# A hybrid attention and delta-rule encoder layer: zero fills on VectorE, some stores and loads issued by ScalarE

## The chip, the core and the metric

The kernel runs on one core of a Trainium2 chip. The metric is the device time of one execution in microseconds (us); less is better. A core has five engines with a queue of instructions each, and each takes its own in order: TensorE (PE, with its weight loads as PEld), VectorE (DVE), ScalarE (ACT), GpSimd (POOL) and SyncE (SP). They wait for each other by semaphores. Transfers (DMA) are issued by an engine and run beside it; SP does nothing else than issue them.

## The reference

One trunk layer on x of 1 x 1024 x 1024 in float32:

```
h   = x + W_out( concat[ windowed attention , gated DeltaNet both ways ] )( RMSNorm(x) )
h   = h + W2 relu(W1 RMSNorm(h))^2
out = RMSNorm_final(h)
```

The attention has 8 query heads and 2 key heads of 64, a window of 128 around each token, and a relative bias from a small table. The DeltaNet has 4 heads of 128, chunks of 64 tokens, and two directions. For each chunk and head it needs the inverse of a unit triangular matrix of 64 x 64 (`t_mat`, below), and then runs a recurrence over the chunks:

```
a_mat = where(strict, beta * kk * decay, 0)
t_mat = triangular_solve(eye + a_mat, eye)
v_new = u - w @ state ;  o = q @ state + qk @ v_new ;  state = state * exp(gl) + k^T @ v_new
```

## The kernel before

The sequence of 1024 tokens is worked on in chunks of 128 (eight, NT) or halves of 512 (HALF). Large gemms (`mm3`, L124 to L126) split each float32 operand into a high part, which is the value rounded to a shorter mantissa, and the low rest, and add three products; `split` (L119 on ACT, L120 on POOL) makes the parts.

The work is written as Python generators (projections, inversion, attention, scan, output, feed-forward) which are woven together. At build a planner then lays every instruction out in one order on each engine, by its own estimate of the times. So an edit of a line, which changes what that line costs in the plan, can move other instructions on every engine, also far behind it. Buffers come from rings: `pg` (128 x 1024), `pt` (128 x 512), `wr`, `wh`, `wl`, `sc`, and the PSUM banks `psA` and `psB`. A number behind such a name is the buffer's place in the program.

What stands around the change:

- `proj_attn` ends with the queries: for each key head kv, two pieces i of the heads and two halves, a gemm into psA, L494 (DVE, scale), L495 (ACT, high part qh), L496 (POOL, low part), and then four stores of 128 KB each into `qad` in HBM (L500): two of the high part, two of the low. There are 32 stores. `query(n, kv)` (L594) reads a chunk of the queries of one key head back, issued by POOL; `attention` uses it in L544 and L545 on PE, followed by the softmax (L546, L553 to L563) and its transposes (L573, L575, L585). Its bias tiles come by L529 from `biasd`.
- The triangular matrices are inverted in blocks. The innermost, 32 x 32, is an elimination on DVE (L675 and L677, then L686 and L687). `invert(tt, steps)` joins the blocks to 64 x 64, for each of four steps i and both directions d. A step loads two tiles of `atd` (L707, 512 KB each), clears two tiles of `tt` (L710), copies the diagonal blocks in (L714, ACT) and then goes back and forth between PE and a copy: L720 (PE), L723 (ACT), L730 and L734 (PE), L739 and L746 (DVE), L744 (ACT), L753 (PE), L755 (ACT), L761 (PE), L764 (DVE).
- `scan` (from L780; its first matmul is L797) begins when the first tiles are inverted.
- Later, `out_gdn(c)` norms the DeltaNet's output of chunk c: squares on ACT (L900), five small operations (L902 to L906, the last on POOL), L907 (DVE, writes a `wr`), L910 (four transposes on PE), L911 (DVE). `out_gemm` multiplies the result by W_out (L124 to L126, added to h by L876). Beside it `tokens_second` makes the second half of the normed tokens: L209 (transposes on PE), L214 and L966 (ACT), L215 and L970 (DVE), L949 (ACT) and L950 (DVE or POOL).

Of the kernel before, what the change touches and what calls it, by code (L numbers as in the profile page):

```python
# [21 lines left out]
HALF = 512  # L22
# [55 lines left out]
class Block:  # L78
# [383 lines left out]
    def proj_attn(self):  # L462


        nc = self.nc
        w = self.io["w_in"][0]
        raws = self.load_w(self.w_cols(w, C_AK, 256))
        lo, up = slice(0, 64), slice(64, 128)
        self.kh, self.kl = [self.pg(dt=F32R) for _ in range(2)], [self.pg(dt=F32R) for _ in range(2)]
        for v, o in enumerate((up, lo)):  # L470
            nc.vector.tensor_copy(out=self.kl[v][o, :], in_=self.zero[o, :].to_broadcast([64, SEQ]))
        self.va = self.pg((P, NT, P))
        for i, half, ps in self.pair(raws):
            tok = slice(half * HALF, (half + 1) * HALF)
            t = self.pt()
            nc.vector.tensor_copy(out=t, in_=ps)
            if i == 0:
                swap = self.pt()
                nc.sync.dma_start(out=swap[up, :], in_=t[lo, :])
                nc.sync.dma_start(out=swap[lo, :], in_=t[up, :])  # L480
                for v, (r, o) in enumerate(((lo, up), (up, lo))):
                    nc.scalar.copy(out=self.kh[v][r, tok], in_=t[r, :])
                    nc.scalar.copy(out=self.kh[v][o, tok], in_=swap[o, :])
                    nc.gpsimd.tensor_tensor(out=self.kl[v][r, tok], in0=t[r, :], in1=self.kh[v][r, tok].bitcast(F32),
                                            op=ALU.subtract)
            else:
                pv = self.transposed(t, 0)
                nc.vector.tensor_copy(out=self.va[:, 4 * half:4 * half + 4, :], in_=pv)
            yield 5.2
        for kv in range(2):  # L490
            raws = self.load_w(self.w_cols(w, C_AQ + 256 * kv, 256))
            for i, half, ps in self.pair(raws):
                q, qh = self.pt(), self.pt(dt=F32R)
                nc.vector.tensor_scalar(out=q, in0=ps, scalar1=0.125, scalar2=None, op0=ALU.mult)  # L494
                nc.scalar.copy(out=qh, in_=q)  # L495
                nc.gpsimd.tensor_tensor(out=q, in0=q, in1=qh.bitcast(F32), op=ALU.subtract)  # L496
                for part, t in enumerate((qh.bitcast(F32), q)):
                    o = 64 * (kv ^ part)
                    for g in range(2):
                        nc.sync.dma_start(out=self.qad[kv, 2 * i + g, o:o + 64, half * HALF:(half + 1) * HALF],  # L500
                                          in_=t[64 * g:64 * g + 64, :])
                if i == 1 and half == 0:
                    self.qs.append(self.query(0, kv))
                yield 5.2
# [186 lines left out]
    def invert(self, tt, steps):  # L691


        nc = self.nc
        blk = lambda q: slice(32 * q, 32 * q + 32)
        ct, ctt = self.ct, self.ctt
        pairs = (((0, 1), (2, 3)), ((1, 0), (3, 2)))
        sub = ((0, 1), (3, 2))
        lo, hi = slice(0, 64), slice(64, 128)
        ends = ((lo, hi), (hi, lo))  # L700
        flat = lambda a: a.rearrange("p c h x -> p (c h) x")
        for i in steps:
            ns = slice(8 * i, 8 * i + 8)
            at = []
            for d in range(2):
                a = self.pg((P, 2, GH, P))
                nc.sync.dma_start(out=a, in_=self.atd[2 * i:2 * i + 2, :, d].rearrange("c p h x -> p c h x"))  # L707
                at.append(flat(a))
                tt[d][i] = self.pg((P, 2, GH, P)) if d or i < 2 else (self.wl if i % 2 else self.wh)((P, 2, GH, P), F32)
                nc.gpsimd.memset(tt[d][i].rearrange("p c h x -> p (c h x)"), 0.0)  # L710
            t = [flat(tt[d][i]) for d in range(2)]
            for d in range(2):
                for q in range(4):
                    nc.scalar.copy(out=t[d][blk(q), :, blk(q)], in_=ctt[d][blk(q), :, ns].rearrange("p x n -> p n x"))  # L714
            px = self.ps("psB", (P, 8, 32))
            for n in range(8):
                for j in range(2):
                    for d in range(2):
                        s, e = pairs[d][j]
                        nc.tensor.matmul(px[blk(e), n, :], at[d][blk(s), n, blk(e)], ct[d][blk(s), :, 8 * i + n],  # L720
                                         start=True, stop=True)
            x32 = self.pt((P, 8, 32))
            nc.scalar.copy(out=x32, in_=px)  # L723
            yield 1.4
            pyt, py = self.ps("psB", (P, 8, 32)), self.ps("psB", (P, 8, 32))
            for n in range(8):
                for j in range(2):
                    for d in range(2):
                        s, e = pairs[d][j]
                        nc.tensor.matmul(pyt[blk(s), n, :], x32[blk(e), n, :], ctt[d][blk(e), :, 8 * i + n],  # L730
                                         start=True, stop=True)
                for d in range(2):
                    e = sub[d][1]
                    nc.tensor.matmul(py[blk(e), n, :], ctt[d][blk(e), :, 8 * i + n], x32[blk(e), n, :],  # L734
                                     start=True, stop=True)
            t64 = self.pt((P, 8, 64))
            for d in range(2):
                for s, e in pairs[d]:
                    nc.vector.tensor_scalar(out=t[d][blk(s), :, blk(e)], in0=pyt[blk(s)], scalar1=-1.0, scalar2=None,  # L739
                                            op0=ALU.mult)  # L740
                a, b = sub[d]
                for q in (a, b):
                    c = slice(32 * (q % 2), 32 * (q % 2) + 32)
                    nc.scalar.copy(out=t64[blk(q), :, c], in_=ct[d][blk(q), :, ns].rearrange("p x n -> p n x"))  # L744
                nc.gpsimd.memset(t64[blk(a), :, 32 * (b % 2):32 * (b % 2) + 32], 0.0)
                nc.vector.tensor_scalar(out=t64[blk(b), :, 32 * (a % 2):32 * (a % 2) + 32], in0=py[blk(b)], scalar1=-1.0,  # L746
                                        scalar2=None, op0=ALU.mult)
            yield 2.4
            px = self.ps("psB", (P, 8, 64))
            for n in range(8):  # L750
                for d in range(2):
                    s, e = ends[d]
                    nc.tensor.matmul(px[e, n, :], at[d][s, n, e], t64[s, n, :], start=True, stop=True)  # L753
            xs = self.pt((P, 8, 64))
            nc.scalar.copy(out=xs, in_=px)  # L755
            yield 1.8
            py = self.ps("psB", (P, 8, 64))
            for n in range(8):
                for d in range(2):
                    s, e = ends[d]  # L760
                    nc.tensor.matmul(py[s, n, :], xs[e, n, :], t[d][e, n, e], start=True, stop=True)  # L761
            for d in range(2):
                s, e = ends[d]
                nc.vector.tensor_scalar(out=t[d][s, :, e], in0=py[s], scalar1=-1.0, scalar2=None, op0=ALU.mult)  # L764
            yield 1.8
# [612 lines left out]
```

## Time and profile before

| what | value |
|---|---|
| median of 3 runs | 1255.21 us (1253.97 to 1259.02) |
| the profiled execution | 1255.02 us |
| its span, first to last instruction | 1253.3 us |
| mean granted TensorE clock | 0.983 |
| busy: PE, PEld, DVE, ACT, POOL | 1191.6, 967.2, 854.9, 621.4, 580.3 us |
| DMA | 187.62 MB, 150 GB/s over the span |
| L710, eight memsets on POOL | 954 to 1088 ns each, from 263.0 to 346.5 us |
| L500, 32 stores issued by SP | 572 ns each in the median, from 298.8 to 342.0 us |
| L707, eight loads issued by SP | 438 ns each in the median, from 257.5 to 343.4 us |

Times in the views are microseconds from the start of the span; "idle before" or a pair in square brackets is how long an engine had stood before an instruction, and what ended that. `x4` is a count of instructions. A name as `pg<-atd` is what is written and what it is read from. A transfer has two times: that which its issue takes on the issuing engine, and that from the issue to its landing.

### The profile page before, as it was taken

What the parts mean: (1) busy time and instruction counts of PE and PEld (TensorE: products, weight loads), DVE (VectorE), ACT (ScalarE), POOL (GpSimd) and SP (SyncE); (2) the same over time, 40 slices, a digit from 0 to 9 for tenths busy, and PEclk for the clock granted to TensorE, in tenths of its full rate; (3) what the DMA queues carried; (4) which work ended last, traced back from release to release, by engine and by line L of the source; (5) the groups of instructions that cost most, each with busy time, mean ns of one, the idle gap of its engine ahead of it and who ended that gap; (6) DMA issues with size and microseconds to landing.
All of it is one profiled execution on the core that took longest, in us unless ns stands there. A gap on an engine that the chain in (4) does not pass through costs nothing.

```text
span 1253.3 us, 18527 instructions
## 1 busy us (share of the span) xinstructions
PE 1191.6 (95%) x6482; PEld 967.2 (77%) x6482; DVE 854.9 (68%) x1528; ACT 621.4 (50%) x1347; POOL 580.3 (46%) x488
## 2 busy tenths in 40 slices
PE   7999999899789989998999999999999999999997
PEld 5778777677568868877788888888777888888885
DVE  5667667982389986676655454544668797886976
ACT  6455688335485752125464554545545434444343
POOL 5354211362432433144573534535445665655595
PEclk9999999899889999998999999999999999999999
DMA  7134344441956678122234344443678624434323
GB/s 239 52 121 133 101 171 140 139 126 40 223 168 158 190 216 296 60 84 85 84 131 159 132 151 143 154 159 134 223 280 280 223 85 167 151 121 148 95 90 135
DMA packets 121630, 187.62 MB, mean 150 GB/s; under 512 B 11043, under 2 KB 64416, under 8 KB 121537
## 3 DMA queue, kind: packets, MB, share of 16 engines
q1 hardware_dynamic: 96708, 152.58, 37.9%
q10 hardware_dynamic: 16381, 29.67, 6.3%
q0 software_dynamic: 8448, 4.20, 1.9%
q8 instruction: 51, 0.84, 0.3%
q14 instruction: 42, 0.34, 0.1%
HBM read 122.39 MB, written 63.49 MB: 148 GB/s over the span
## 4 chain that ended last, share of the span: by engine, by line
PE 49%; DVE 6%; DMA 3%; issue 2%; POOL 1%; ACT 1%; ACTq 0%; POOLq 0%; DVEq 0%; SPq 0%
PE psA L124 8%; PE psA L125 8%; PE psA L126 8%; PE psB L126 7%; PE psB L125 7%; PE psB L124 7%; DMA pg<-sd 3%; PE psB L797 2%; DVE pg L1154 1%; DVE pt L1163 1%; DVE wr L1166 1%; PE psB L209 1%; DVE pg L1199 1%; DMA sd<-pt 0%; DVE wr L1161 0%
## 5 line engine op out<-in xcount | busy, mean ns | idle before, releaser
L124 PE MATMUL psA<-pg,wh 128*128 128x512 f32 x416 | 167.6, 404 | 2.1 <-ACT pt L458 2.1
L126 PE MATMUL psA<-pg,wl 128*128 128x512 f32 x416 | 166.9, 401 | 0.0
L125 PE MATMUL psA<-pg,wh 128*128 128x512 f32 x416 | 166.5, 400 | 0.0
L120 POOL TENSOR_TENSOR wl<-wr,wh 128x512 fp32r<-128x512 f32 x44 | 70.2, 1618 | 154.0 <-ACT wh L119 153.9
L1154 DVE TENSOR_TENSOR pg<-pg 128x512 fp32r<-128x512 f32 x112 | 122.7, 1127 | 18.8 <-ACT pg L1153 18.6
L120 POOL TENSOR_TENSOR wh<-wr,wh 128x512 fp32r<-128x512 f32 x32 | 47.9, 1518 | 131.5 <-ACT wh L119 131.5
L1071 ACT ACTIVATE pt<-pt 128x512 f32<-128x512 f32 x64 | 40.4, 632 | 122.7 <-DVE pt L1061 122.7
L125 PE MATMUL psA<-pg,pg 128*128 128x512 f32 x256 | 99.7, 391 | 0.5 <-POOL pg L120 0.5
L124 PE MATMUL psA<-pg,pg 128*128 128x512 f32 x256 | 99.0, 391 | 1.0 <-DVE pg L1199 1.0
L126 PE MATMUL psA<-pg,pg 128*128 128x512 f32 x256 | 99.7, 389 | 0.0
L120 POOL TENSOR_TENSOR pg<-wr,pg 128x512 fp32r<-128x512 f32 x48 | 73.4, 1560 | 51.0 <-ACT pg L119 51.0
L124 PEld LDWEIGHTS psA<-pg,wh 128*128 128x128 f32 x416 | 79.2, 190 | 21.3 <-ACT pt L458 2.4
L125 PEld LDWEIGHTS psA<-pg,wh 128*128 128x128 f32 x416 | 79.3, 191 | 19.7 <-issue 0.9
L126 PEld LDWEIGHTS psA<-pg,wl 128*128 128x128 f32 x416 | 79.1, 190 | 18.6
L1153 ACT CAST pg<-pg 128x512 fp32r<-128x512 f32 x112 | 67.2, 620 | 41.3 <-DMA pg<-sd 31.0
L126 PE MATMUL psB<-pg,pg 128*128 128x512 f32 x192 | 75.0, 390 | 1.3 <-DVE pg L1154 1.3
L125 PE MATMUL psB<-pg,pg 128*128 128x512 f32 x192 | 75.0, 391 | 0.8 <-POOL pg L120 0.7
L124 PE MATMUL psB<-pg,pg 128*128 128x512 f32 x192 | 74.7, 390 | 0.4 <-ACT pg L1153 0.4
L119 ACT CAST wh<-wr 128x512 fp32r<-128x512 f32 x76 | 43.6, 623 | 45.5 <-PE psA L125 24.8
L1061 DVE TENSOR_TENSOR pt<-psB,pt 128x512 f32<-128x512 f32 x39 | 26.9, 689 | 55.1 <-PE psB L126 30.1
L1061 DVE TENSOR_TENSOR pt<-psA,pt 128x512 f32<-128x512 f32 x39 | 26.8, 689 | 55.0 <-PE psA L126 39.5
L124 PEld LDWEIGHTS psA<-pg,pg 128*128 128x128 f32 x256 | 48.0, 188 | 12.6 <-DVE pg L1199 2.3
(385 smaller groups left out, 3307.7 us busy)
## 6 DMA issues: line engine op xcount, KB each, us to landing
sd<-pt ACTq DMA_DIRECT2D x112, 256.0 KB, 2.2
pg<-sd SPq DMA_DIRECT2D x112, 256.0 KB, 2.9
wr<-in_w_ffn_in SPq DMA_DIRECT2D x32, 512.0 KB, 3.8
wr<-in_w_in SPq DMA_DIRECT2D x22, 512.0 KB, 4.8
pg<-in_x SPq DMA_DIRECT2D x16, 512.0 KB, 5.4
wr<-in_w_ffn_out SPq DMA_DIRECT2D x16, 512.0 KB, 4.8
sc<-kvd SPq DMA_DIRECT2D x14, 512.0 KB, 4.1
kvd<-pt SPq DMA_DIRECT2D x16, 256.0 KB, 2.8
```

What stands on the lines that cost most here:

```text
L119: nc.scalar.copy(out=h, in_=raw)
L120: (eng or nc.gpsimd).tensor_tensor(out=l, in0=raw, in1=h.bitcast(F32), op=ALU.subtract)
L124: nc.tensor.matmul(ps, wh, xh, start=first, stop=False, skip_group_check=onto)
L125: nc.tensor.matmul(ps, wh, xl, start=False, stop=False, skip_group_check=onto)
L126: nc.tensor.matmul(ps, wl, xh, start=False, stop=last, skip_group_check=onto)
L209: self.nc.tensor.transpose(ps[:, i * P:(i + 1) * P], row[:, k * P:(k + 1) * P], self.ident)
L797: nc.tensor.matmul(ps[:, h - g.start, :], left(h), right[:, h, :], start=True, stop=True)
L1061: self.nc.vector.tensor_tensor(out=out, in0=in0, in1=in1, op=ALU.add)
L1071: self.nc.scalar.activation(out=c, in_=c, func=AF.Relu)
L1153: nc.scalar.copy(out=s[:, 0], in_=raw)
L1154: v.tensor_tensor(out=s[:, 1], in0=raw, in1=s[:, 0].bitcast(F32), op=ALU.subtract)
L1163: v.tensor_tensor(out=b["T2"], in0=b["B22"], in1=b["T1"], op=ALU.subtract)
```

## The change

Three lines change. The stores of the high part of the queries (part 0) are issued by ACT and those of the low part by SP, so 16 of the 32 move. The loads of `atd` for the steps i = 2 and 3 are issued by ACT, so 4 of the 8 move. The eight memsets of 128 x 1024 float32 in `invert` are given to DVE instead of POOL.

```diff
@@ proj_attn
                     for g in range(2):
-                        nc.sync.dma_start(out=self.qad[kv, 2 * i + g, o:o + 64, half * HALF:(half + 1) * HALF],
+                        (nc.scalar, nc.sync)[part].dma_start(out=self.qad[kv, 2 * i + g, o:o + 64, half * HALF:(half + 1) * HALF],
                                           in_=t[64 * g:64 * g + 64, :])
@@ invert
                 a = self.pg((P, 2, GH, P))
-                nc.sync.dma_start(out=a, in_=self.atd[2 * i:2 * i + 2, :, d].rearrange("c p h x -> p c h x"))
+                (nc.sync if i < 2 else nc.scalar).dma_start(out=a, in_=self.atd[2 * i:2 * i + 2, :, d].rearrange("c p h x -> p c h x"))
                 at.append(flat(a))
                 tt[d][i] = self.pg((P, 2, GH, P)) if d or i < 2 else (self.wl if i % 2 else self.wh)((P, 2, GH, P), F32)
-                nc.gpsimd.memset(tt[d][i].rearrange("p c h x -> p (c h x)"), 0.0)
+                nc.vector.memset(tt[d][i].rearrange("p c h x -> p (c h x)"), 0.0)
```

The planner's order changes with it, on each engine. On DVE, around the second step of the inversion (pg_2752 and pg_2756 are its two tiles of `tt`, pt_2969 and those after it are query tiles, pg_3229 is a tile of the third step):

```order
 L739 TENSOR_SCALAR pg_2752<-psB_2801 32x8x32 x2
 L746 TENSOR_SCALAR pt_2851<-psB_2802 32x8x32 x2
+L710 MEMSET pg_2756 128x1024
 L739 TENSOR_SCALAR pg_2756<-psB_2801 32x8x32 x2
 L494 TENSOR_SCALAR pt_2969<-psA_2944 128x512
 L494 TENSOR_SCALAR pt_3003<-psA_2978 128x512
+L710 MEMSET pg_3229 128x1024
+L764 TENSOR_SCALAR pg_2752<-psB_2925 64x8x64
+L764 TENSOR_SCALAR pg_2756<-psB_2925 64x8x64
 L494 TENSOR_SCALAR pt_3047<-psA_3022 128x512
```

The clearing of pg_2756 stands directly ahead of the operation that first writes into it, and L764 of this step ahead of the third query tile instead of behind the fourth. On POOL the same memset stood behind a load of queries:

```order
 L745 MEMSET pt_2851 32x8x32 x2
 L496 TENSOR_TENSOR pt_2895<-pt_2895,pt_2896 128x512
 L594 DMA pt_2904<-qad 128x4x128
-L710 MEMSET pg_2756 128x1024
 L496 TENSOR_TENSOR pt_2969<-pt_2969,pt_2970 128x512
 L496 TENSOR_TENSOR pt_3003<-pt_3003,pt_3004 128x512
```

It is gone from there, and the low parts follow the load directly. On ACT, a little later (pg_3223 and pg_3227 are the tiles of `atd` for the third step, pt_2970, pt_3004, pt_3048 and pt_3088 are high parts of queries):

```order
 L755 COPY pt_2923<-psB_2906 128x512
+L707 DMA pg_3223<-atd 128x2x512
 L495 CAST pt_2970<-pt_2969 128x512
+L707 DMA pg_3227<-atd 128x2x512
+L500 DMA qad<-pt_2970 64x512 x2
 L495 CAST pt_3004<-pt_3003 128x512
+L714 COPY pg_3229<-sc_2482 32x8x32 x4
+L500 DMA qad<-pt_3004 64x512 x2
 L495 CAST pt_3048<-pt_3047 128x512
+L500 DMA qad<-pt_3048 64x512 x2
 L495 CAST pt_3088<-pt_3087 128x512
+L500 DMA qad<-pt_3088 64x512 x2
```

Two loads, the stores and the copies of one tile of the third step now stand between the casts. Far behind, on DVE in `out_gdn` of chunk 0 (wr_5995 is what L907 writes, psA_6010 what L910 makes of it; the other rows are `tokens_second`):

```order
-L907 TENSOR_TENSOR wr_5995<-pg_3794,sm_5998 128x512
+L903 TENSOR_SCALAR sm_5997<-sm_5997 128x4
 L950 TENSOR_TENSOR pg_6140<-pg_6085,pg_6140 128x512
+L904 RECIPROCAL sm_5997<-sm_5997 128x4
 L215 SCALAR_TENSOR_TENSOR pg_6169<-psB_6164,cols,pg_6169 128x512
 L970 SCALAR_TENSOR_TENSOR pg_6143<-psB_6164,cols,pg_6143 128x512
-L911 SCALAR_TENSOR_TENSOR wr_5994<-psA_6010,cols,wr_5995 128x512
+L905 TENSOR_TENSOR sm_5997<-sm_5997,sq_1234 128x4
 L215 SCALAR_TENSOR_TENSOR pg_6197<-psB_6192,cols,pg_6197 128x512
 L970 SCALAR_TENSOR_TENSOR pg_6176<-psB_6192,cols,pg_6176 128x512
 L950 TENSOR_TENSOR pg_6201<-pg_6143,pg_6201 128x512
+L907 TENSOR_TENSOR wr_5995<-pg_3794,sm_5998 128x512
```

L907 moves behind the last groups of `tokens_second`. PE's row of L910 is where it was, ahead of the gemm of chunk 1:

```order
L209 MATMUL psB_6192<-ident,pg_5076 128x128
L209 MATMUL psB_6192<-ident,pg_4973 128x128
L910 MATMUL psA_6010<-ident,wr_5995 128x128 x4
L124 MATMUL psA_6020<-pg_5224,pt_5870 128x512
L125 MATMUL psA_6020<-pg_5225,pt_5870 128x512
```

These five rows stand in this order before and after.

## The prediction

> **What bounds the kernel now.** I read the first page for the busiest engine, then the table of waits of 255 to 395 us, where the changed lines run, then the timeline there, and last the place far behind it where the built order differs.
>
> ```profile
> PE 1191.6 (95%) x6482; PEld 967.2 (77%) x6482; DVE 854.9 (68%) x1528; ACT 621.4 (50%) x1347; POOL 580.3 (46%) x488
> ```
>
> PE is busy for 1191.6 of 1253.3 us, so a saving elsewhere counts only where PE stands still for it, and each new standstill of PE counts whole. The columns of the next two views are the waiting engine and line, what ended the wait, the sum, the count and the longest.
>
> ```profile
> POOL pt L594 <- DMA pg<-biasd: 12.6, 2, 8.7
> ACT pg L714 <- POOL pg L710: 8.1, 2, 7.3
> DVE pg L739 <- POOL pg L710: 6.0, 1, 6.0
> PE psB L761 <- ACT pt L755: 4.9, 2, 4.4
> ```
>
> One memset (L710) is waited for by ACT for 7.3 us and by DVE for 6.0, and one wait of PE is 4.4. The timeline shows that they are one event:
>
> ```profile
> 316.05 0.40 PE L125 MATMUL psA<-pg,wh 128*128 128x512 f32 x1
> 316.28 0.40 PE L126 MATMUL psA<-pg,wl 128*128 128x512 f32 x1
> 316.61 1.15 PE L753 MATMUL psB<-pt,pg 64*64 64x64 f32 x32
> 316.94 1.00 POOL L594 DMA_DIRECT2D pt<-qad  x1 [3.89 <-DMA pg<-biasd]
> 317.95 0.97 POOL L710 MEMSET pg<- 128x1024 f32 x1
> 318.95 2.51 ACT L714 COPY pg<-sc 32x256 f32<-32x256 f32 x4 [7.32 <-POOL pg L710]
> 318.95 0.88 DVE L739 TENSOR_SCALAR pg<-psB 32x256 f32<-32x256 f32 x2 [6.02 <-POOL pg L710]
> 321.48 0.59 ACT L755 COPY pt<-psB 128x512 f32<-128x512 f32 x1
> 322.12 1.68 PE L761 MATMUL psB<-pg,pt 64*64 64x64 f32 x32 [4.36 <-ACT pt L755]
> ```
>
> POOL is in order: its query load waits for transfers, the memset stands behind it, L714 behind the memset, L755 behind L714, and PE stands from 317.76 to 322.12.
>
> The standstill costs twice, since the clock falls behind it (the busy columns are PE, PEld, DVE, ACT and POOL; the last three are PEclk, DMA share and GB/s):
>
> ```profile
> 322.00:324.00 2.00, 1.88 (x33) 1.76 (x34) 0.50 (x2) 1.98 (x5) 1.21 (x1) 0.63 0.54 154
> 324.00:326.00 2.00, 2.00 (x6) 1.56 (x7) 1.22 (x2) 0.27 (x1) 2.00 (x3) 0.52 0.88 199
> 340.00:346.00 6.00, 4.36 (x167) 3.96 (x167) 2.71 (x15) 5.93 (x16) 3.95 (x7) 0.50 1.31 337
> 585.00:588.60 3.60, 3.60 (x19) 3.60 (x18) 3.19 (x8) 3.29 (x8) 1.02 (x1) 0.50 0.00 0
> ```
>
> From 322 to 326 the mean granted clock is (0.63 + 0.52) / 2 = 0.58: some 3.4 us at half speed, as 4 us x 0.42 / 0.5 gives. Half of that, 1.7 us, is what such a stretch costs a PE that is never idle in it. The Trainium skill, page "TensorE: Matmul & The Clock Gate", section "What's actually happening", has a half clock after an idle window of about 3.4 us, in windows that run free of the kernel; the rows agree in length, and a free phase is why I give each clock term a range from zero.
>
> The second half of the stage waits for stores. Here SP's own queue and the transfers' readers, and at the end the landing of L529's loads and of L500's stores:
>
> ```profile
> 314.48 7.28 SPq L529 DMA_DIRECT2D pg<-biasd  x14
> 322.74 11.30 SPq L500 DMA_DIRECT2D qad<-pt  x16
> 334.08 1.07 SPq L529 DMA_DIRECT2D pg<-biasd  x2
> 335.25 0.89 SPq L707 DMA_DIRECT2D pg<-atd  x2
> 335.74 0.40 PE L126 MATMUL psA<-pg,wl 128*128 128x512 f32 x1
> 336.52 0.79 POOL L594 DMA_DIRECT2D pt<-qad  x1 [8.72 <-DMA pg<-biasd]
> 339.60 0.28 PE L720 MATMUL psB<-pg,pg 32*32 32x32 f32 x2 [2.12 <-DMA pg<-atd]
> 342.76 0.55 PE L544 MATMUL psA<-pg,pt 128*128 128x256 f32 x1 [0.82 <-DMA pt<-qad]
> DMA to landing us min/median/max: 2.1/2.7/3.1
> DMA to landing us min/median/max: 2.2/2.4/5.4
> ```
>
> The last of sixteen stores leaves SP at 334.08; with the median landing of L500 (the last row) it is there at 336.5, which is when POOL goes on with the load of query(0,1) (its releaser is inferred). PE uses that query at 342.76, 6.24 us after the issue, though its gemms ended at 336.14.
>
> **The change, part by part.** These rows carry the prices:
>
> ```profile
> L710 POOL MEMSET pg<- x6: 954/964/1088, 263.0 to 346.5; 128x1024 f32 x6
> L205 DVE TENSOR_SCALAR pg<-pg,sm x12: 744/754/1755, 6.8 to 582.2; 128x1024 f32<-128x1024 f32 x12
> L471 DVE CAST pg<-zero x2: 684/1185/1686, 268.7 to 270.4; 64x1024 fp32r<-64x1024 f32 x2
> L500 SPq DMA_DIRECT2D qad<-pt x32: 445/572/1702, 298.8 to 342.0; - x32
> L707 SPq DMA_DIRECT2D pg<-atd x8: 360/438/537, 257.5 to 343.4; - x8
> ```
>
> *Memsets.* POOL loses 8 x 0.96 = 7.7 us; it is 46% busy, so that alone is worth nothing. DVE has no such memset before. The nearest row is L205, the same 128x1024 f32 on the same engine: I take 0.75 us, with 0.68 (the fastest L471) and 1.19 (its mean) as the ends: 6.0 us, 5.4 to 9.5. The Trainium skill, page "VectorE: DVE Perf Modes", section "Zero memsets can be issued as uint32 (trn2)", states a cycle for each element of a memset; with the 0.96 GHz that its page "Trainium Kernel Development and Optimization" gives that is an estimate of 1.07 us, so 8.5 us, above the row that I take; the sum below would be the same, since none of the eight ends on PE's path. The first two now stand inside the elimination (L675/L677), which ends some 1.5 to 2.4 us later; PE does ten gemm matmuls ahead of its L720 instead of behind them (0.23 us apart, as at 316.05 and 316.28, so 2.3 us), which hides it. Without that cover up to 2.4 us would be lost; I keep it in the lower end of the gain.
>
> The fourth, pg_2756, is the one of the timeline. DVE is free from 312.9 (318.95 - 6.02), so it clears there by 313.7; L714 then runs at 313.7 to 316.2, and L755 waits only for PE's L753, which ends at 317.76. L761 follows at some 318.4, or at 317.9 with a half microsecond gained ahead of it, in place of 322.12: 3.7 to 4.2 us, I take 4.0. The stretch at half clock behind it goes too: 0 to 1.7 us, I take 1.4. So the projections' last gemm ends at 336.14 - 5.4 = 330.7.
>
> *Stores and loads issued by ACT.* Sixteen stores and four loads leave SP: 16 x 0.57 + 4 x 0.44 = 10.9 us of issue. ACT takes that on, and is in order: ACT's two loads for i=2 stand ahead of its casts (L495), and they wait for transfers already under way to land (bias loads, of which SP issues fourteen by 321.76 and which land 2.1 to 3.1 later, so from some 320 to 324), so the casts of the tiles behind them wait too. L714 of pg_3229 (2.51) also moves ahead of two of these casts. I walk the fourth cast (pt_3088) to about 329, POOL's L496 and SP's two stores to 332, and their landing of 2.4 to 334.4. The query load then leaves at 334.4 instead of 336.52, 2.1 earlier, and lands 4.8 to 6.24 later: PE's L544 at 339.2 to 340.6, so 2.1 to 3.5 us earlier than 342.76. The atd loads are no longer the wait, since ACT has issued them early: L720 comes ahead, at about 333. Of the 5.4 us that PE had won it gives back about half, standing from some 333 to 340: **the removed wait on the memset returns as a wait for the query.**
>
> Behind that ACT is the bound (5.93 of 6 us busy from 340 to 346), and some 7 us of its work there (L714, the first exponentials) is then done sooner, so what PE has won is kept, and the scan starts that much earlier. What reaches the scan: **gain 2.9 us**, between 1.0 (the elimination or ACT's queue late by two) and 5.4 (the query early enough).
>
> *The order far behind.* Nothing of the edit is there, yet DVE's order at the last out_gdn (c=0) moves: L903 to L907 now stand between and behind the operations of tokens_second. In the trace:
>
> ```profile
> 585.58 3.90 PE L209 MATMUL psB<-ident,pg 128*128 128x128 f32 x20
> 588.73 0.68 DVE L907 TENSOR_TENSOR wr<-pg,sm 128x512 f32<-128x512 f32 x1
> 589.33 0.68 DVE L950 TENSOR_TENSOR pg<-pg,pg 128x512 fp32r<-128x512 f32 x1
> 589.46 0.66 PE L910 MATMUL psA<-ident,wr 128*128 128x128 f32 x4
> 589.93 0.74 DVE L215 SCALAR_TENSOR_TENSOR pg<-psB,cols,pg 128x512 fp32r<-128x512 f32 x1
> 590.06 0.69 ACT L214 ACTIVATE pg<-psB,cols 128x512 fp32r<-128x512 f32 x1
> 590.59 0.74 DVE L970 SCALAR_TENSOR_TENSOR pg<-psB,cols,pg 128x512 f32<-128x512 f32 x1
> ```
>
> L907 writes what PE's L910 reads, and PE, before and after, has L910 directly behind the last L209, ahead of 24 and more gemm matmuls. Before, L907 is over at 589.41 and PE goes on at 589.46. After, L907 has ahead of it on DVE: L950 and L215 and L970 of the last but one group (L215 starts at about 589.8, since its ACT half ends then), then L215, L970 of the last group (not before L214's end at 590.75) and another L950. From 589.8: 0.75 + 0.74 + 0.15 (L905) + 0.74 + 0.75 + 0.68 + 0.68 = 594.3. PE waits from 589.48 to 594.2: 4.7 us, between 4.0 (DVE some 0.7 ahead, having put off four small operations) and 5.0. The page's PE share and this stage's DVE (3.19 of 3.60) say that nothing absorbs it: behind it come PE's own gemms. PE then stands longer than at 317.76, so a stretch at half clock follows: 1.7, between 0 and 2.9. **Loss 6.4 us**, 4.0 to 7.9.
>
> *The rest.* In the FFN single rows change places (L1061 against L1036, some matmuls); the waits there are between other lines, and I count zero, with half a microsecond to both sides.
>
> **Sum.** The profiled execution took 1255.02 us (its span is 1253.3), 0.19 under the median 1255.21. 1255.0 - 2.9 + 6.4 = **1258.5**: a little slower, which is inside 0.5% (6.3 us, so 1248.9 to 1261.5), about what a measurement of this kernel can tell from no change.
>
> **The rivals.**
> 1. *Slower: ACT's queue swallows the gain.* The loads for i=2 wait on ACT ahead of the casts; for each microsecond that they hold ACT beyond about 323 the stores of the last tiles, and query(0,1), come later. If the query load leaves at 336.5 or later, there is no gain: it decides when the fourth cast starts after 331. For it: L594's wait of 8.7 us is on a transfer, and ACT now has more of the chain. Against it: SP has half of its sixteen stores less. Time: 1255.0 + 6.4 = 1261.4, or 1262.6 with a clock loss of 2.9. Here belongs the rule of the Trainium skill, page "DMA: Bandwidth & Descriptors", section "Issuing engines are not separate DMA queues", by which issuing from another engine saves only the issue time; the 10.9 us of issue are no wait of PE by themselves. Chance 0.20.
> 2. *No loss at 589.* DVE reaches L907 in time if tokens_second comes much earlier than out_gdn needs it. Against it: L214's end at 590.75 stands ahead in DVE's order. Time: 1255.0 - 2.9 = 1252.1. Chance 0.12.
> 3. *The gain whole, with the loss.* The query is there by 334; against it are the 4.8 us of landing: 1255.0 - 5.4 + 6.4 = 1256.0. Chance 0.10.
> 4. *Both good* (2 and 3): 1249.6. Chance 0.06.
>
> **How the numbers follow.** My forecast, 1256.5 to 1260.5, has the remaining 0.52. From 1251.5 to 1263.0 hold the forecast and rivals 1, 2 and 3 and leave out rival 4 and tails of some 0.12 in all. Faster by over 0.5% is a part of rival 4 alone: 0.04. Slower by over 0.5% is most of rival 1 and a tail of the forecast: 0.18. Within: 0.78.
>
> **What would show it.** In the changed profile: no wait of ACT L714 or DVE L739 for L710 above a microsecond, MEMSET rows of L710 on DVE of 0.7 to 1.2; L761 of step 1 at about 318; the last gemm of the projections near 331; PE's L544 waiting on qad for several us; the first L797 some 3 us earlier; and PE L910 of c=0 waiting on DVE L907 for 4 to 5 us, with half clock behind it. I am wrong if that last wait is under 1 us, or if L544 comes at 342 or later. If PE's path has another place where the order turns, which I saw none of, the sum fails.

## The result and the profile after

| kernel | median | runs | ratio to before, 95% interval |
|---|---|---|---|
| before | 1256.94 us (1253.97 to 1262.98) | 9 | |
| changed | 1264.09 us (1260.41 to 1266.86) | 9 | 1.0052 (1.0037 to 1.0068) |

The change makes the kernel slower by about 6.5 us (0.52% of 1256.9; by its interval, 4.7 to 8.5). The forecast was 1258.5, the range ended at 1263.0. The profiled execution of the changed kernel took 1260.41 us, the fastest of its nine, with a span of 1258.7; the one of before, 1255.02, also lies 1.9 below the median in the table.

The first line of the page, and the rows on the two changed operations (line, engine, form, duration minimum, median and maximum in ns, first and last start; of L500 and L707 the issue on each queue):

```profile
PE 1189.1 (94%) x6482; PEld 964.8 (77%) x6482; DVE 857.1 (68%) x1536; ACT 621.6 (49%) x1347; POOL 573.0 (46%) x480
...
L710 DVE MEMSET pg<- x6: 912/912/912, 270.8 to 348.4; 128x1024 f32 x6
L707 ACTq DMA_DIRECT2D pg<-atd x4: 370/428/992, 317.6 to 343.6; - x4
L500 ACTq DMA_DIRECT2D qad<-pt x16: 452/489/614, 301.4 to 336.9; - x16
```

The work is the same and PE is not busier; it stands longer. Where it stands, first around the changed lines, by the timeline of the changed kernel (start, duration, engine, line; in brackets the time stood before it and what ended it):

```profile
314.80 0.40 PE L753 MATMUL psB<-pt,pg 64*64 64x64 f32 x8
315.89 0.92 PE L761 MATMUL psB<-pg,pt 64*64 64x64 f32 x24 [0.69 <-ACT pt L755]
...
328.00 0.39 PE L126 MATMUL psA<-pg,wl 128*128 128x512 f32 x1
...
336.00 0.79 POOL L594 DMA_DIRECT2D pt<-qad  x1 [4.14 <-DMA qad<-pt]
340.19 0.55 PE L544 MATMUL psA<-pg,pt 128*128 128x256 f32 x1 [9.64 <-DMA pt<-qad]
...
374.75 1.37 PE L797 MATMUL psB<-sc,sc 128*128 128x128 f32 x8 [1.24 <-DVE sc L815]
```

The wait of 4.36 us at 317 is down to 0.69. The projections' last gemm matmul (L126) ends at 328.39, where it ended at 336.14 before. L720 and a few L544 and L545 follow, up to 330.55, and then PE stands for 9.64 us for a query. The scan's first wait, which ended at 376.49 before, ends at 374.75: 1.74 us are left. Then, far behind:

```profile
590.83 0.48 PE L910 MATMUL psA<-ident,wr 128*128 128x128 f32 x1 [4.01 <-DVE wr L907]
...
912.25 0.50 PE L124 MATMUL psA<-pg,sc 128*128 128x512 f32 x1 [1.35 <-ACT pt L1066]
```

PE waits 4.01 us for L907, where it had not waited. The last row is a landmark in the feed-forward: 905.82 before, 912.25 after. From the scan's landmark to this one the kernel before takes 529.3 us and the changed one 537.5.

The clock by stretches, of the changed kernel and, as the second pair, of a second profile of it (`again` below); the columns are as in the prediction, PEclk third from the right:

```profile
590.00:597.00 7.00, 6.17 (x18) 5.04 (x19) 1.68 (x4) 0.84 (x2) 2.88 (x2) 0.55 0.34 104
627.00:634.00 7.00, 6.25 (x16) 4.83 (x17) 5.50 (x9) 6.59 (x13) 6.29 (x6) 0.51 0.00 0
```
```profile
590.00:597.00 7.00, 4.72 (x13) 3.89 (x14) 2.97 (x5) 1.50 (x3) 3.67 (x3) 0.56 0.21 66
627.00:634.00 7.00, 5.42 (x17) 4.07 (x18) 5.79 (x9) 6.23 (x12) 6.11 (x6) 0.60 0.00 0
```

Both stretches had a clock of 1.00 in the profile of before. The first lies directly behind the new wait. The second does not, and the runs with L907 early show below that it is not a part of the slowdown.

### The profile page after: what moved, and what is told of

Read it like the earlier page. It is cut to its first block, busy times and chain, and to the rows that moved or that the text cites. A ratio compares the mean times of both kernels' runs of the same rounds, so it can differ in the third digit from the quotient of the medians.

```text
span 1258.7 us, 18510 instructions
## 1 busy us (share of the span) xinstructions
PE 1189.1 (94%) x6482; PEld 964.8 (77%) x6482; DVE 857.1 (68%) x1536; ACT 621.6 (49%) x1347; POOL 573.0 (46%) x480
## 5 line engine op out<-in xcount | busy, mean ns | idle before, releaser
L126 PE MATMUL psA<-pg,wl 128*128 128x512 f32 x416 | 166.1, 399 | 0.0
L126 PE MATMUL psA<-pg,pg 128*128 128x512 f32 x256 | 99.6, 389 | 0.0
L126 PEld LDWEIGHTS psA<-pg,wl 128*128 128x128 f32 x416 | 78.6, 189 | 18.4
L126 PE MATMUL psB<-pg,pg 128*128 128x512 f32 x192 | 74.7, 389 | 0.0
```

The lines of the kernel that those rows point to most:

```text
L126: nc.tensor.matmul(ps, wl, xh, start=False, stop=last, skip_group_check=onto)
```

## The experiments

The table puts the runs together. "L797" is the end of the scan's first wait, in us; "stretch" is from there to the feed-forward's landmark, each of one profile; the ratio is to the kernel before, with its interval. M, S and L are the three parts: memsets on DVE, high stores on ACT, loads on ACT. "Half" is an L907 that stands two operations earlier than late. Each of these edits moves the planner's order too, so a row is a kernel and not an issuing engine alone.

| label | parts | L907 of c=0 | PE's wait at L910 | L797 | stretch | ratio |
|---|---|---|---|---|---|---|
| before | none | early | none | 376.5 | 529.3 | |
| b_f | none, scratch edit | early | none | 375.7 | 531.8 | 1.0006 (0.9992 to 1.0019) |
| changed | M S L | late | 4.0 | 374.8 | 537.5 | 1.0052 (1.0037 to 1.0068) |
| again | M S L | late | 4.1 | 376.0 | 537.4 | 1.0052 (1.0032 to 1.0072) |
| sub_pool | M S L | half | 3.2 | 375.8 | 535.6 | 1.0042 (1.0028 to 1.0057) |
| msl_f | M S L, scratch edit | early | none | 374.5 | 531.7 | 1.0004 (0.9993 to 1.0016) |
| ml | M L | late | 4.2 | 375.3 | 535.7 | 1.0043 (1.0030 to 1.0056) |
| m | M | late | 4.2 | 375.5 | 537.2 | 1.0039 (1.0024 to 1.0054) |
| m_f | M, scratch edit | early | none | 374.6 | 534.5 | 1.0010 (0.9999 to 1.0020) |
| ms | M S | late | 4.2 | 372.8 | 537.4 | 1.0011 (0.9990 to 1.0032) |
| ms_f | M S, scratch edit | early | none | 370.6 | 532.7 | 0.9981 (0.9971 to 0.9991) |
| msg_f | M S, loads for i=2 by POOL, scratch edit | early | none | 374.8 | 533.0 | 0.9999 (0.9979 to 1.0018) |
| s_f | S, scratch edit | early | none | 377.8 | 531.3 | 0.9997 (0.9977 to 1.0016) |

The stretch parts the kernels without an overlap: 535.6 to 537.5 us where L907 is late or half, 529.3 to 534.5 where it is early, 4.8 us between the means. L797 is a weaker sign: it differs by 1.3 us between two profiles of one kernel, changed and again.

**again**: the changed kernel, unaltered.

> The changed kernel itself once more, for what differs from one execution to the next. Theory A (the late L907 of out_gdn, c=0: 4.0 us of standing and some 2.6 us of half clock behind it) and theory B (the half-clock stretches fall where a free phase puts them, and decide the rest) both expect the same waits: PE's L910 of c=0 waits 3.8 to 4.2 us, PE's L544 for qad 9 to 10 us, the scan's first waits within 0.5 us of the first profile. B alone expects the stretches at half clock behind 590 us (590 to 597 and 627 to 634 in the first profile) to differ by one of 3.4 us or more, with a time that differs from 1260.4 by 2 us or more; A by itself expects them in the same places and a time within 1 us.

The waits are nearly the same, 4.08 at L910 and, a little over the 9 to 10 expected, 10.35 at L544; the scan's first wait ends 1.26 us later, also outside of what was expected. The span is 2.7 us longer, 1261.4 against 1258.7. Summed over windows of 1 us from 200 to 1245 us, the half clock lasts 34.1 us in the first profile and 47.8 in this one; a stretch costs up to half its length where PE has work. So one profile of this kernel is uncertain by some 2 to 3 us from the clock alone. Theory B is right on that for single profiles (the stretches at 590 and 628 are in both, others are new, at 348 and 966); the comparison of medians stays at 1.0052 both times, so it does not explain the slowdown.

**sub_pool**: the subtractions of tokens_second leave DVE's queue.

```diff
-                self.operand("T3", self.t3[k - 1], k % 2)
+                self.operand("T3", self.t3[k - 1], 0)
```

> The changed kernel, with the subtractions L950 of tokens_second all on POOL. In the order only 16 rows of DVE and 10 of POOL move; L907 then stands behind L970 of the last group but one, two DVE operations earlier and without an L950 ahead. Theory A: PE's L910 of c=0 waits 1.3 to 2.0 us instead of 4.0 and the time is 2.3 to 5 us under the changed kernel's (the half clock behind it is shorter or gone). Theory C (the stores and loads on ACT cost the time, the wait at L910 is absorbed behind): the wait gets shorter but the time stays within 1 us of the changed kernel's.

The wait went from 4.0 only to 3.16 us, since L907 still stood behind L970 of the last group but one; 1.3 to 2.0 was too hopeful. The ratio, 1.0042, cannot be told from 1.0052. It settles nothing.

**ml** and **m**: single parts of the change.

```diff
# ml: the change without the stores; m: the memsets alone
-                        (nc.scalar, nc.sync)[part].dma_start(out=self.qad[kv, ...
+                        nc.sync.dma_start(out=self.qad[kv, ...
# m, also:
-                (nc.sync if i < 2 else nc.scalar).dma_start(out=a, ...
+                nc.sync.dma_start(out=a, ...
```

> The memsets on DVE and the loads for i=2 and 3 on ACT, but all stores on SP again. In the planner's order L907 of c=0 is then where it was before the change; on PE 14 rows differ from the changed kernel's. Theory A: no wait of PE for L907 above 0.5 us at c=0; what is gained up to the scan (0 to 3 us) stays: time 1254 to 1257.5, that is 5 to 9 us under the changed kernel's. Theory C: the gain up to the scan is larger than the changed kernel's 1.7 us by 4 us or more, since the stores no longer load ACT, and the difference is made ahead of 380 us, not at 590.

> The memsets alone on DVE; stores and loads on SP as before. In the planner's order L907 of c=0 is late as in the changed kernel. Theory A: PE's L910 of c=0 waits 3.5 to 4.5 us, the last gemm of the projections ends at 330 to 331.5, but the query load leaves when SP's sixteen stores have landed (336 to 337), so PE stands for 11 to 13 us and the scan starts 0 to 1.5 us earlier than before; time 1261 to 1266, as the changed kernel or up to 2 us more. Theory C: without stores and loads on ACT the time is that of before or less, 1253 to 1258.

The premise of ml was wrong: in its order L907 is as late as in the changed kernel. The waits of PE from 575 to 700 us say so, of ml:

```profile
PE psA L910 <- DVE wr L907: 4.2, 1, 4.2
```

So ml did not test what it was built for. What it and m do show: with M alone, and with M and L, the scan starts about as early as with all three (375.5, 375.3), the wait at L910 is there, and the time is 1.0039 and 1.0043. Theory C, by which the stores and loads on ACT cost the time, expected m at or below the kernel before, and fell. In m the query load left at 332.9 us, not at 336 to 337, and PE waited for the loads of atd (8.0 us at L720), not for the query as expected; its scan started within 1 us of the changed kernel's all the same.

**msl_f** and **b_f**: L907 early again, in the changed kernel and, as a control, in the one before. The four squares of out_gdn(0) write to one scratch tile, each over the last; with a slice for each they depend no more on each other, and the planner puts the small operations behind them together and L907 early. On PE the edit also moves L910 ahead of the last four transposes L209, in both kernels alike. The kernel computes the same.

```diff
-        scr = self.small((P, P), bufs=2, tag="scr")
+        scr = (lambda s: [s[:, h] for h in range(GH)])(self.pt((P, GH, P))) if c == 0 else [self.small((P, P), bufs=2, tag="scr")] * GH
...
-            nc.scalar.activation(out=scr, in_=o[:, h, :], func=AF.Square, accum_out=so[:, h:h + 1])
+            nc.scalar.activation(out=scr[h], in_=o[:, h, :], func=AF.Square, accum_out=so[:, h:h + 1])
```

> The changed kernel, with the scratch of the four squares L900 of out_gdn(0) taken as four slices of a pt tile instead of one tile that each of them overwrites. In the order nothing moves ahead of 570 us; there L902 to L905 stand directly behind L205 and L907 ahead of the second pair of L215 and L970, as early as before the change or earlier. Theory A (the late L907 is the whole of the loss): PE's L910 of c=0 waits under 0.7 us and the time is 4.5 to 8 us under the changed kernel's, so 1255 to 1258.5, at or just below that of before. Theory C (the loss is made elsewhere, and the wait at L910 is only where it shows): the wait goes, another takes its place behind, and the time stays above 1260.5.

> The kernel before, with the same edit of the scratch and nothing else: the control. L907 of c=0 is early in it as it was. Theory A: the time is that of before within 2 us (the edit itself is worth nothing), no wait of PE for L907 above 0.3 us. If it is faster by 4 us or more, then the edit brings something of its own, and the fall of the other kernel says nothing on L907.

The timeline of msl_f at the place, and its clock in the two stretches of above and in one between them:

```profile
585.22 0.68 DVE L907 TENSOR_TENSOR wr<-pg,sm 128x512 f32<-128x512 f32 x1
586.94 0.60 PE L910 MATMUL psA<-ident,wr 128*128 128x128 f32 x4
...
590.00:597.00 7.00, 7.00 (x32) 5.68 (x31) 2.43 (x4) 1.15 (x2) 1.30 (x3) 1.00 0.65 218
620.00:628.00 8.00, 6.11 (x19) 4.54 (x20) 6.50 (x11) 7.27 (x14) 7.34 (x7) 0.57 0.00 0
627.00:634.00 7.00, 7.00 (x30) 5.69 (x29) 3.98 (x5) 5.52 (x12) 7.00 (x6) 0.96 0.26 79
```

L907 is over a microsecond before PE comes to L910, nothing is waited for, the half clock behind L910 is gone, and the ratio falls from 1.0052 to 1.0004: 6.0 us, with an uncertainty of some 2.4 from the two intervals. The other half clock is not gone: it only comes earlier, at 620 to 628 (0.57), and the control has it at 622 to 629 (0.51). It lies behind short waits of PE's L209 for DVE's L993, which every one of these kernels has. All six with the scratch edit show the half clock there; of the seven profiles without the edit, changed, again and sub_pool do, and before, ml, m and ms do not. So it goes neither with the late L907 nor with the early one. The control is at 1.0006, so the edit brings nothing of its own. **The slowdown is the late L907**, by its wait and the half clock directly behind it. The pair msl_f and b_f also says what the three parts are worth without it: 1.0004 against 1.0006, nothing that can be measured, with an uncertainty of some 2.2 us.

**ms_f** and **m_f**: which part gave back the gain, with L907 early.

```diff
# ms_f: msl_f with the loads on SP;  m_f: also the stores on SP
-                (nc.sync if i < 2 else nc.scalar).dma_start(out=a, ...
+                nc.sync.dma_start(out=a, ...
```

> The memsets on DVE and the high parts' stores on ACT, all loads of atd on SP, with the scratch edit. Theory Q (ACT's queue, held by the loads' and stores' waits for earlier transfers, is what makes the query late): without the two loads ahead of the casts, the load of query(0,1) leaves 2 to 5 us earlier than the changed kernel's 336.0, PE's wait for it at 331 shrinks from 9.6 to 4.5 to 8 us, the scan starts 1.5 to 4 us earlier; time 1251 to 1256. Rival (the atd loads on SP come too late, and L720 waits instead): PE stands as long, at L720 for atd, the scan starts within 1 us of the changed kernel's; time 1254.5 to 1258.5.

> The memsets alone on DVE, with the scratch edit. Theory A: as the memsets-only kernel, but without the wait at L910 of c=0, so 4.5 to 8 us below its 1262.2: 1254 to 1258. The scan starts as there (1 us before that of the kernel before); the time against before is -2 to +1.

The casts L495 of ACT on pt_2970, pt_3004, pt_3048 and pt_3088, between and behind the two loads, of the changed kernel and then of ms_f:

```profile
318.20 0.62 ACT L495 CAST pt<-pt 128x512 fp32r<-128x512 f32 x1 [2.36 <-DMA pg<-biasd]
323.81 0.62 ACT L495 CAST pt<-pt 128x512 fp32r<-128x512 f32 x1 [5.00 <-DVE pt L494]
328.03 0.62 ACT L495 CAST pt<-pt 128x512 fp32r<-128x512 f32 x1 [1.01 <-DMA pg<-atd]
329.90 0.62 ACT L495 CAST pt<-pt 128x512 fp32r<-128x512 f32 x1 [1.25 <-DVE nm L546]
```
```profile
316.00 0.62 ACT L495 CAST pt<-pt 128x512 fp32r<-128x512 f32 x1
321.37 0.62 ACT L495 CAST pt<-pt 128x512 fp32r<-128x512 f32 x1 [4.75 <-DMA qad<-pt]
323.85 0.62 ACT L495 CAST pt<-pt 128x512 fp32r<-128x512 f32 x1 [1.86 <-DMA qad<-pt]
326.38 0.62 ACT L495 CAST pt<-pt 128x512 fp32r<-128x512 f32 x1 [1.91 <-DMA qad<-pt]
```

Without the two loads the first of these casts starts 2.2 us earlier and the fourth 3.5. Not all of that is the loads' waits: L714 (2.67 us on ACT) stands ahead of the third cast in the changed kernel and behind the fourth in ms_f. The query load leaves at 334.8 (336.0), 1.2 us earlier and not the 2 to 5 expected. PE's wait for it shrinks to 1.95, with 4.3 at L720 for atd ahead of it, as the rival had it in part:

```profile
PE psB L720 <- DMA pg<-atd: 4.3, 2, 2.6
PE psA L544 <- DMA pt<-qad: 2.2, 2, 1.9
```

The scan starts 4 us earlier than in the changed kernel, and the ratio is 0.9981 (0.9971 to 0.9991): 2.4 us faster than before, the only one of these kernels that beats both. Of the 4 us, 1.9 are there when PE comes to L544 (338.31 against 340.19); the others are made behind it, where the order differs too, and no run says by what. So theory Q is borne out in its direction, loads on ACT delay the casts behind them, but not in its sizes. m_f, at 1.0010, is not faster than before, and with 1258.27 just above what was expected; its profile has an unusual 51.2 us at half clock. With M, then, S pays only without L: m_f is at 1.0010, msl_f at 1.0004, and ms_f at 0.9981. What S brings there is not the query, whose load leaves at 334.87 in m_f and at 334.79 in ms_f: with half of the stores gone from SP, the loads of atd leave it at 325.4 and 327.3 instead of from 333.2 on, and PE's wait at L720 falls from 7.6 to 4.3 us.

**msg_f**, **s_f** and **ms**: the loads on a third queue, the stores alone, and ms_f with L907 late.

```diff
# msg_f, from ms_f:
-                nc.sync.dma_start(out=a, ...
+                (nc.gpsimd if i == 2 else nc.sync).dma_start(out=a, ...
# s_f, from ms_f:
-                nc.vector.memset(tt[d][i]...
+                nc.gpsimd.memset(tt[d][i]...
# ms: ms_f without the edit of the scratch
```

> As ms_f (memsets on DVE, high stores on ACT, scratch edit), with the two loads of atd for i=2 issued by POOL, ahead of its low parts L496, instead of by SP. Theory Q (in-order queues that carry a transfer's wait hold up the casts and low parts that the query needs): ACT is as free as in ms_f; L720 of i=2 waits for atd under 1 us instead of 4.3; the time is 1 to 4 us under ms_f's, 1250 to 1253. Rival (the loads' waits only change queue): POOL's L496 come late by the loads' waits as ACT's casts did, query(0,1) leaves at 336 or later, PE waits 8 us or more at L544 and the time is msl_f's, 1255 to 1258.

> Only the high stores on ACT, with the scratch edit; memsets on POOL and loads on SP as before. If the memset on DVE is worth what it saves ahead of 331 us, this kernel has PE's wait of 4.4 us at 317 (L761 for ACT L755 for POOL's memset) and is 1.5 to 4 us slower than ms_f: 1255.5 to 1258. If the query's way through HBM alone sets the scan's start, the wait at 317 is made good at 331 to 340, and the time is ms_f's within 1 us, 1253 to 1255.

> ms_f without the scratch edit: in the planner's order L907 of c=0 is late again, with nothing else of the edit changed ahead of 570 us. Theory A: PE's L910 of c=0 waits 3.5 to 4.5 us, the scan starts as in ms_f, and the time is 4.5 to 7.5 us over ms_f's 1254.05: 1258.5 to 1261.5.

On POOL the loads leave at 317.6, early enough that L720 does not wait, but the query load leaves at 337.1 and PE waits 8.4 us at L544: the rival held, the time is msl_f's (0.9999). s_f keeps the wait at 317 (here 4.34, up to 325.2). Its scan starts 7 us after ms_f's, but 2.9 of them are there at 224 us already, where PE's wait for L458 ends, ahead of all changed lines. In time it is 0.9997, 2.0 us over ms_f, as the first expectation had it; its interval touches ms_f's, so what M is worth beside S is not settled. ms has L907's wait back (4.2) and a stretch 4.7 us longer than ms_f's; the ratio rises from 0.9981 to 1.0011, 3.8 us, less than the 4.5 to 7.5 expected, with an interval of ms that is too wide to say more. Its scan starts at 372.8, not at 370.6 as in ms_f, though the two have one order up to there: so some 2 of ms_f's 4 us may be that execution's own.

## Why the prediction was wrong, by its steps

*The memsets.* The price, 0.75 us by the row of L205, was too low: 0.912 in all eight. That is between the ends given (0.68 to 1.19), and below the estimate of 1.07 from the Trainium skill's page "VectorE: DVE Perf Modes", section "Zero memsets can be issued as uint32 (trn2)". It changed nothing: they stand on no path, and the elimination's extra time was hidden as expected (no wait at L720 near 281 any more).

*The wait at 317 and the end of the gemms.* The wait went and the half clock behind it went, as forecast. The size was too small: L761 came at 315.9 (forecast "317.9 or 318.4") and the last gemm ended at 328.39, 328.96 in the second profile (forecast 330.7). PE had won 7.2 to 7.8 us there, not 5.4. One source that the sum did not count is the wait of L720 for L687, 1.61 us at 282 before and gone after.

*The query.* That the wait comes back at L544 was right (9.64, at 330.55 to 340.19; forecast 333 to "339.2 to 340.6"; the second profile, at 341.47, is outside). L720 came at 328.8, not at about 333. The query load left at 336.0, and at 337.3 in the second profile, not at 334.4. The fourth cast was put at 329 and started at 329.90; the stores issued from 320 to 342 us took 2.8 us to land in the median, at most 5.0, where I had used 2.4.

*"What PE has won is kept."* This is **the step that failed**, with the late query ahead of it: together they are the term "gain 2.9 us". PE came to L544 2.6 us (first profile) or 1.3 us (second) earlier than before, and the scan starts only 1.74 or 0.5 us earlier, so some 0.8 us of the lead is lost behind L544 in both. I had taken ACT to be busy from 340 on with some 7 us of its work done early. The timeline after shows it standing:

```profile
343.14 0.21 ACT L555 ACTIVATE nm<-nm 128x4 f32<-128x4 f32 x1 [4.68 <-DVE nm L554]
```

ACT's work done early was followed by a wait that ends with the very query that PE waited for. That this wait is what took the 0.8 us is argued; no run tests it alone. The clock does not explain it: PE comes back from its 9.6 us at half clock, up to 344 us, but the profile of before has the half clock there too, and for longer (339 to 347 and 349 to 357). **Gain: forecast 2.9 us, measured 0.3 by the pair msl_f and b_f** (1.0004 against 1.0006, uncertain by some 2.2), about 1 by the scan's start (375.3 in the mean of the four profiles with this order, against 376.1 in the two with that of before). That is rival 1, ACT's queue swallows the gain, to which I had given 0.20, for the greater part: its sign for no gain, a query load at 336.5 or later, came in the second profile only, and its other sign, a fourth cast after 331, did not come; at 329.9 most of the gain was gone already.

*The order far behind.* Right in place, in mechanism and nearly in size: PE's wait at L910 is 4.0 to 4.2 us (forecast 4.7, 4.0 to 5.0), a half clock follows, and the whole is 6.0 us (forecast 6.4, 4.0 to 7.9) by the pair changed and msl_f; by the pairs m and m_f, ms and ms_f it is 3.6 and 3.8, each with an uncertainty of over 2. So the loss is shown, and its size is 4 to 6 us. The rule on the clock of the Trainium skill's page "TensorE: Matmul & The Clock Gate", section "What's actually happening" (a half clock after an idle window of about 3.4 us, the windows free of the kernel), agrees in length and in phase: the dips last 3.4, 6.8, 10.2 or 13.7 us, and changed and ms have the same waits for L993 (1.00 and 1.35 us, 0.98 and 1.35), but only changed has a half clock behind them. It does not agree on the idle window: in msl_f PE had stood for only 0.56 and 1.35 us, with transposes between, when the half clock of 620 to 628 began.

*The base.* The sum was built on one execution of 1255.02. The median of nine is 1256.94, and the stretch between the landmarks, 529.3 us, is the shortest of all profiles with an early L907 (531.3 to 534.5 in the others): it had fewer stretches at half clock than usual, 10 us from the scan to the landmark against 14 to 20 in the others. With the base of 1256.9, no gain and 6.0 to 6.4 of loss, the sum would be 1263; the median measured is 1264.1. So of the 5.6 us between forecast and measurement, 1.9 are the base and 2.6 the gain; the rest is within the spread. That the time was forecast as slower at all rests on the loss, whose mechanism was right.

*The rivals.* No loss at 589 (2), and both good (4), are refuted by the wait. The whole gain (3) is refuted by the query, which was not there by 334.

*The rule on issuing engines.* m_f and ms_f differ in S alone, 1.0010 against 0.9981, 3.6 us. The Trainium skill, page "DMA: Bandwidth & Descriptors", section "Issuing engines are not separate DMA queues", allows for a gain in issue time only. These runs don't contradict it: S frees SP for the loads of atd (above). That L costs 2.9 us (msl_f against ms_f) fits with what then stands behind the loads' waits in ACT's queue, but L's edit moves L714 as well.

## What to carry to other kernels

Where a planner lays out the order at build, an edit pays or costs also where it was not made: compare the order on each engine to the end of the program, and look for an instruction of the bound engine whose producer has moved behind other work; here one DVE operation some 250 us behind the edit cost 4 to 6 us, more than the best of these edits brought (2.4). A transfer's issue put on a computing engine can be a wait on that engine: with the loads on ACT, two of them ahead of the casts, what the stores on ACT had won was gone. A sum that is made against a single profile inherits what that execution was lucky in; look at the spread of the runs first. And a window at fixed times can lose a stretch that has only moved: compare by what the engine was doing.

## What was not expected of the hardware

The memset of 128x1024 float32 took 912 ns on DVE in every one of eight instances, and 954 to 1088 on POOL: DVE hardly wins there, though a TENSOR_SCALAR of that shape took 754 on DVE in the median. Two profiles of one program, whose waits at L544 and L910 agree to 0.8 us, differed by 13.7 us in their time at half clock and by 2.7 us in span, in a kernel whose PE is 94% busy.
